# A trunk of two layers on one core: outputs turned in another PSUM bank, seven query buffers, and a norm by Sqrt

## The chip, the cores and the metric

The kernel runs on one core of a Trainium2 chip. A core has a matrix engine (TensorE, PE in the profile; PEld is its load of weights), a vector engine (VectorE, DVE), a scalar engine (ScalarE, ACT), GpSimd (POOL) and an engine whose queue issues most DMAs (SyncE, SP). Each engine runs its own queue in order; semaphores tie the queues together. Matrix products land in PSUM, which has eight banks of 128 x 512 fp32; everything else lies in SBUF. The metric is the device time of one launch in microseconds (us), as the median of several runs.

## The reference

One sequence of 512 tokens, 1024 channels, fp32, goes through two layers.

```python
# layer 0
h = rmsnorm(x, norm_mix[0])
x = x + hgrn2_mixer(h, ...)                 # gated linear recurrence, 8 heads of 128 x 128
x = x + conv_ffn(rmsnorm(x, norm_ffn[0]))   # up 1024 -> 5632, causal conv of 3, silu gate, down 2816 -> 1024
# shared keys and values
kv = rmsnorm(x, kv_norm) @ kv_w
# layer 1
h = rmsnorm(x, norm_mix[1])
x = x + diff_attention(h, k, v, ...)        # 8 heads, two softmaxes each: p1 - lam * p2
x = x + conv_ffn(rmsnorm(x, norm_ffn[1]))
return rmsnorm(x, final_norm)               # y = x * rsqrt(mean(x * x) + EPS) * g
```

In the mixer `q = silu(q)`, `f` is squashed into a forget gate between a learned lower bound and 1, and the head's output at a token is the sum over earlier tokens of `q . k`, each channel weighted by the product of the forget gates in between. In attention each head has two query-key products with a relative-position bias; `attn = p[0] - lam * p[1]` meets the values, and the 128 outputs of a head are normalised (`b_subln`) before the last projection.

## The kernel before

Activations are kept transposed: channels on the 128 partitions, the 512 tokens along a row, eight tiles `x0` to `x7`. An fp32 product is made of three products of a faster format: `split` (L59, L60) takes a tile apart into a high and a low part, ACT makes the high one and DVE the low one, and `mm3` (L99 to L101) issues three matrix products of up to 512 columns. So each weight block (512 KB, three buffers, fetched by SP's queue) costs a cast on ACT, a subtraction on DVE and 24 products on PE.

**The mixer** (`hgrn`) goes head by head. Each head's projections are followed by `prep`, a long run of elementwise work, almost all on DVE, that makes queries and keys decayed to the start or end of blocks of 4, 16, 32, 64 and 128 tokens. The query tiles of the last four lie in one pool with the tag "Q" and `QB` buffers (`QB` is 3). A tile of twice the block is made of the one before: ACT copies one half (L406), DVE multiplies the other by the gates' product (L407). `intra` then issues on PE the many small products of a head's blocks (L423, L425, then L430, L434, L437 for blocks of 16, 32, 64), transposes the keys (L445), makes the states (L450), and DVE gathers the parts under masks (L468, L479). ACT copies them to `scd` (L482 to L487), and the head's output is made by L490 (with `scd`) and L492 (with the 128-token query tile and the state). The order of all this is not written by hand: a scheduler sets each engine's queue from the dependences and the free buffers, so the number of buffers moves instructions.

**Attention** is written in an order by hand (`manual_schedule`). PSUM has four kinds of banks here: `mm` (2) for projections, `sc` (4) for scores, `tp` (1) for transposes, `po` (1) for a head's output. A head has four blocks of 128 queries. An iteration of the loop issues: the two score products of the block two ahead (`scores`, L976 and L977; DVE adds the bias and takes the row's extreme, L979; ACT takes the exponential, L985), one unit of projections on PE (three products of 512 columns), the softmax weights of the block one ahead on DVE (`weigh`, L1000), the transposes of the current block's weights into the bank `tp` (`turn`, L1007) with ACT's copy to `aT` (L1009), one or two more units, the product with the values (`gather`, L1020), and another unit. Once a head is complete, `close` normalises its output, and in the second block of the next head `turn_back` transposes it (L1037); ACT and DVE split the result into `yh` (L1039) and `yl` (L1040). `turn_back` uses the one `tp` bank, so the `turn` that comes after it waits until `yl` has been read out.

**The last norm** (`last_tile`) works on two halves of 256 tokens of the last tile, and PE does the second half's products while the first half is finished. `factor` makes 1/rms of the tokens, as a column of 128 tokens each, from sums of squares: an integer trick gives a start (L607), and three Newton steps on DVE follow, each of two instructions for each of two columns (L614, L617). `spread` transposes the columns to rows (L183), and `finish` multiplies the tiles, scaled beforehand on ACT by the norm's gain (`scaled`, L588), and sends them out (L640).

Of the kernel before, what the change touches and what calls it, by code (L numbers as in the profile page):

```python
# [11 lines left out]
F32 = mybir.dt.float32  # L12
F32R = mybir.dt.float32r
I32 = mybir.dt.int32
AF = mybir.ActivationFunctionType
# [6 lines left out]
D = 1024  # L22
# [2 lines left out]
DFF = 2816  # L25
KF = DFF // P
EPS = 1e-6
KB, QB = 6, 3
ORDERED = {mybir.EngineType.PE, mybir.EngineType.DVE, mybir.EngineType.Activation, mybir.EngineType.Pool}
U1, U2, U3 = 2, 3, 1  # L30
PIECES = {0: 1, 1: 3, 3: 6, 6: 8}
# [5 lines left out]
class Trunk:  # L37
# [530 lines left out]
    def last_tile(self, w_src, ys, kt, acc, out):  # L568

        nc, v, sp = self.nc, self.nc.vector, self.sp  # L570
        ws = []
        for k0 in range(0, kt, 8):
            wd = min(8, kt - k0)
            ws.append(self.weights(w_src[:, k0 * P:(k0 + wd) * P], wd * P))
        x, last = self.x, KD - 1
        t = [slice(half * 256, half * 256 + 256) for half in range(2)]
        ps = [self.bank() for _ in range(2)]
        sq = [sp.tile([P, T], F32, tag="sq", name="sq", bufs=2) for _ in range(2)]

        def product(half, ks):  # L580
            for k in ks:
                hi, lo = ws[k // 8]
                c = slice(k % 8 * P, k % 8 * P + P)
                self.mm3(ps[half][:, :256], (hi[:, c], lo[:, c]), (ys[k][0][:, t[half]], ys[k][1][:, t[half]]),
                         k == 0, k == kt - 1)

        def scaled(n, c):
            nc.scalar.activation(xg[n][:, c], x[n][:, c], AF.Identity, scale=self.gain(5, n))  # L588

        def squares(half):  # L590
            c = t[half]
            v.tensor_tensor(x[last][:, c], x[last][:, c], ps[half][:, :256], ALU.add)
            nc.scalar.activation(sq[half][:, c], x[last][:, c], AF.Square)
            scaled(last, c)

        def tmp(dt=F32):
            return sp.tile([P, 4], dt, tag="rs", name="rs", bufs=18)[:, :2]

        def sums(src, half):
            return self.sums(src, "mm", (2 * half, 2 * half + 1))[:, 2 * half:2 * half + 2]  # L600

        def factor(half):

            ss = sums(sq[half], half)
            ms, mh, i = tmp(), tmp(), tmp(I32)
            v.scalar_tensor_tensor(ms, ss, 1.0 / D, before[half], ALU.mult, ALU.add)
            v.tensor_scalar(i, ms.bitcast(I32), -0.5, float(0x5F3759DF), ALU.mult, ALU.add)  # L607
            v.tensor_scalar(mh, ms, -0.5, None, ALU.mult)
            r = i.bitcast(F32)
            for step in range(3):  # L610
                u, rn = tmp(), tmp()
                for c in range(2):
                    c = slice(c, c + 1)
                    v.scalar_tensor_tensor(u[:, c], r[:, c], mh[:, c], r[:, c], ALU.mult, ALU.mult)  # L614
                for c in range(2):
                    c = slice(c, c + 1)
                    v.scalar_tensor_tensor(rn[:, c], u[:, c], 1.5, r[:, c], ALU.add, ALU.mult)  # L617
                r = rn
            return r

        def spread(r):

            both = [self.bank() for _ in range(2)]
            for rb in both:
                for c in range(2):
                    self.by_column(rb[:, c * P:(c + 1) * P], r[:, c:c + 1])
            return both

        def finish(half, rb):
            by_pool = (KD - 2, KD - 1) if half else (KD - 3, KD - 2, KD - 1)  # L630
            rs = sp.tile([P, T], F32, tag="rbc", name="rbc_fin")
            nc.scalar.copy(rs[:, :256], rb[1][:, :256])
            y = [self.xp.tile([P, 2, 256], F32, tag="xs", name="fin", bufs=2 * KD) for _ in range(KD // 2)]
            for n in by_pool:
                nc.gpsimd.tensor_tensor(y[n // 2][:, n % 2], xg[n][:, t[half]], rs[:, :256], ALU.mult)
            for n in range(by_pool[0]):
                v.tensor_tensor(y[n // 2][:, n % 2], xg[n][:, t[half]], rb[0][:, :256], ALU.mult)
            queues = (nc.sync, nc.scalar if half else nc.sync)
            for n in range(0, KD, 2):
                queues[n // 2 % 2].dma_start(out[n:n + 2, :, t[half]].rearrange("n p t -> p n t"), y[n // 2])  # L640

        with self.tc.manual_schedule(engines=ORDERED):
            xg = [self.xp.tile([P, T], F32, tag="xs", name="xg", bufs=2 * KD) for _ in range(KD)]
            product(0, range(kt))
            for n in range(last):
                scaled(n, slice(0, T))
            squares(0)
            product(1, range(4))
            before = [tmp() for _ in range(2)]
            for half in range(2):  # L650
                v.tensor_scalar(before[half], sums(acc, half), 1.0 / D, EPS, ALU.mult, ALU.add)
            r = factor(0)
            product(1, range(4, kt - 6))
            rb = spread(r)
            finish(0, rb)
            product(1, range(kt - 6, kt))
            squares(1)
            finish(1, spread(factor(1)))


    def ffn(self, layer, xs, acc, on_tile, final=None):
# [66 lines left out]
    def attention(self, xkv, acc, on_tile):  # L728
# [3 lines left out]
        with ExitStack() as ctx:  # L732
# [292 lines left out]
            def close(h):  # L1025

                sums, r0, ms, po = heads.pop(h)
                o = self.sp.tile([P, T], F32, tag="res", name="o", bufs=1)
                me = self.sp.tile([P, 4], F32, tag="ome", name="ome")
                r = self.sp.tile([P, 4], F32, tag="or", name="or")  # L1030
                by_token = o.rearrange("p (i x) -> p i x", i=4)

                def turn_back():
                    tp = self.bank("tp")
                    for i in range(4):
                        oi = slice(i * P, (i + 1) * P)
                        nc.tensor.transpose(tp[:, oi], o[:, oi], self.ident)  # L1037
                    hi, lo = ys[h]
                    s.activation(hi, tp, AF.Identity, scale=self.subg2)  # L1039
                    v.scalar_tensor_tensor(lo, tp, self.subg2, hi.bitcast(F32), ALU.mult, ALU.subtract)  # L1040

                s.copy(o, po)
                chain.append(lambda: v.tensor_scalar(me, ms, 1.0 / P, EPS, ALU.mult, ALU.add))
                chain.extend(self.rsqrt_steps(r, me, 4))
                chain.append(lambda: v.tensor_tensor(r, r, r0, ALU.mult))
                chain.append(lambda: v.tensor_tensor(by_token, by_token, r.unsqueeze(2).broadcast_to([P, 4, P]),
                                                     ALU.mult))
                return turn_back
# [242 lines left out]
```

## Time and profile before

| | us |
|---|---|
| median of three timed runs | 1247.64 |
| lowest and highest of them | 1247.16, 1250.83 |
| the profiled execution's own time | 1250.46 |
| its span, first to last instruction | 1248.6 |
| PE busy in the span | 1230.5 |
| DVE busy | 842.9 |
| ACT busy | 576.0 |

In the span the mixer takes roughly the first 260 us, the first feed-forward layer runs to about 640, attention to about 865, the second feed-forward layer and the last norm to the end. A matrix product is counted as busy from its start to its modelled end, and several are in flight at once, so a busy PE need not be one at its peak. Where a row ends in brackets, it tells how long the engine stood idle before the instruction and which instruction's end released it. The trace gives the clock that TensorE was granted, as a share of the full one.

### The profile page before, as it was taken

Reading aid. Unit: us, or ns where it says so; the run is one execution under the profiler, and the core shown is the slowest. Engines: PE = TensorE matmul, PEld = TensorE weight load, DVE = VectorE, ACT = ScalarE, POOL = GpSimd, SP = SyncE. Lnnn points to the kernel's source line nnn. Section 1 sums busy time; section 2 is a strip of 40 time slices with the busy share of each in tenths; the row PEclk is TensorE's granted clock in tenths of the full one; section 3 lists DMA queues with packets and bytes.
Section 4 is the critical chain, followed back from the end, with each engine's and each line's share of the span. In section 5 each row is a group of like instructions: output and inputs, shape, how many; then the busy total and the mean of one; then the engine's idle time right before and its main releaser. Section 6 shows DMA issues by size and latency. Waiting matters only on the chain.

```text
span 1248.6 us, 17998 instructions
## 1 busy us (share of the span) xinstructions
PE 1230.5 (99%) x6994; PEld 1042.3 (83%) x6994; DVE 842.9 (68%) x1659; ACT 576.0 (46%) x1001; POOL 10.1 (1%) x32
## 2 busy tenths in 40 slices
PE   9999999999999999999999999999999999999997
PEld 7888898888888888888888888888888888888886
DVE  6988879686777777633356877777687777762223
ACT  6564555454444444322345666654444444442221
POOL 0000000000000000000000000000000000000001
PEclk9999999999999999999999999999999999999999
DMA  6233222232333332333323322213232332333322
GB/s 231 69 86 121 86 62 75 69 106 98 100 88 99 102 99 89 91 94 101 100 86 114 90 85 68 86 68 94 90 105 88 99 101 99 89 91 95 104 81 68
DMA packets 39613, 117.46 MB, mean 94 GB/s; under 512 B 4280, under 2 KB 10216, under 8 KB 39528
## 3 DMA queue, kind: packets, MB, share of 16 engines
q1 hardware_dynamic: 38488, 115.37, 29.9%
q8 instruction: 55, 0.90, 0.3%
q10 hardware_dynamic: 1040, 0.94, 0.2%
q14 instruction: 30, 0.25, 0.1%
HBM read 112.09 MB, written 3.68 MB: 93 GB/s over the span
## 4 chain that ended last, share of the span: by engine, by line
PE 62%; issue 30%; DVE 5%; ACT 2%; DMA 1%; POOL 0%; SPq 0%; POOLq 0%; ACTq 0%; DVEq 0%
PE mm L101 18%; PE mm L99 18%; PE mm L100 17%; PE po L1020 1%; DVE wlo L60 1%; PE tp L1007 1%; PE sc L99 1%; PE sc L100 1%; PE sc L101 1%; PE sc L977 1%; PE sc L976 1%; PE at L490 1%; DVE wlo L772 0%; DMA raw<-in_w_fqg_dram 0%; DVE sc L979 0%
## 5 line engine op out<-in xcount | busy, mean ns | idle before, releaser
L99 PE MATMUL mm<-xh,whi 128*128 128x512 f32 x944 | 371.3, 394 | 0.8 <-ACT whi L59 0.7
L100 PE MATMUL mm<-xl,whi 128*128 128x512 f32 x944 | 368.7, 391 | 0.6 <-DVE xl L63 0.5
L101 PE MATMUL mm<-xh,wlo 128*128 128x512 f32 x944 | 368.1, 390 | 0.0
L60 DVE TENSOR_TENSOR wlo<-wst,whi 128x1024 fp32r<-128x1024 f32 (+1 forms) x172 | 206.3, 1202 | 146.3 <-ACT whi L59 144.1
L59 ACT CAST whi<-wst 128x1024 fp32r<-128x1024 f32 (+1 forms) x172 | 177.1, 1033 | 240.4 <-PE mm L100 185.3
L100 PEld LDWEIGHTS mm<-xl,whi 128*128 128x128 f32 x944 | 177.6, 188 | 37.6 <-DVE xl L63 2.1
L99 PEld LDWEIGHTS mm<-xh,whi 128*128 128x128 f32 x944 | 177.6, 188 | 37.4 <-ACT whi L59 1.3
L101 PEld LDWEIGHTS mm<-xh,wlo 128*128 128x128 f32 x944 | 177.4, 188 | 37.0 <-DVE wlo L60 0.2
L99 PE MATMUL mm<-hh,whi 128*128 128x512 f32 (+1 forms) x374 | 141.0, 377 | 0.0
L100 PE MATMUL mm<-hl,whi 128*128 128x512 f32 (+1 forms) x374 | 140.8, 377 | 0.0
L101 PE MATMUL mm<-hh,wlo 128*128 128x512 f32 (+1 forms) x374 | 140.8, 376 | 0.0
L679 DVE TENSOR_TENSOR u<-mm,rbc_f 128x512 f32<-128x512 f32 x88 | 60.2, 688 | 73.4 <-PE mm L101 73.4
L99 PEld LDWEIGHTS mm<-hh,whi 128*128 128x128 f32 x374 | 70.4, 188 | 13.0
L100 PEld LDWEIGHTS mm<-hl,whi 128*128 128x128 f32 x374 | 70.4, 188 | 13.0
L101 PEld LDWEIGHTS mm<-hh,wlo 128*128 128x128 f32 x374 | 70.4, 188 | 12.7
L681 ACT ACTIVATE c<-u,pack 128x512 f32<-128x512 f32 x88 | 71.5, 817 | 7.5 <-DVE u L679 3.6
L59 ACT CAST hh<-c 128x512 fp32r<-128x512 f32 x44 | 27.3, 619 | 103.0 <-DVE c L690 103.0
L99 PE MATMUL mm<-whi,xh 128*128 128x256 f32 x248 | 71.7, 289 | 0.0
L101 PE MATMUL mm<-whi,xl 128*128 128x256 f32 x248 | 70.2, 283 | 0.0
L100 PE MATMUL mm<-wlo,xh 128*128 128x256 f32 x248 | 70.0, 282 | 0.0
L683 DVE SCALAR_TENSOR_TENSOR c<-u,pack,c 128x512 f32<-128x512 f32 x88 | 66.1, 751 | 2.7
L682 DVE SCALAR_TENSOR_TENSOR c<-u,pack,c 128x512 f32<-128x512 f32 x88 | 65.4, 745 | 0.0
(280 smaller groups left out, 1691.4 us busy)
## 6 DMA issues: line engine op xcount, KB each, us to landing
wst<-in_w_up_dram SPq DMA_DIRECT2D x88, 512.0 KB, 3.6
wst<-in_w_down_dram SPq DMA_DIRECT2D x32, 512.0 KB, 3.5
wst<-in_w_fqg_dram SPq DMA_DIRECT2D x21, 512.0 KB, 3.8
wst<-in_w_kq_dram SPq DMA_DIRECT2D x16, 512.0 KB, 3.6
wst<-in_w_down_dram SPq DMA_DIRECT2D x16, 384.0 KB, 3.1
wst<-in_w_i_dram SPq DMA_DIRECT2D x8, 512.0 KB, 3.9
wst<-in_w_ao_dram SPq DMA_DIRECT2D x8, 512.0 KB, 4.3
wst<-in_w_v_dram SPq DMA_DIRECT2D x8, 512.0 KB, 3.6
```

Of the source, the lines that this page charges most:

```text
L59: i = nc.scalar.copy(hi, x)
L60: j = nc.vector.tensor_tensor(lo, x, hi.bitcast(F32), ALU.subtract)
L99: mm(out, s[0], m[0], start=start, stop=False)
L100: mm(out, s[0], m[1], start=False, stop=False)
L101: mm(out, s[1], m[0], start=False, stop=stop)
L490: mm(ch(po, j), vh(j), sct[:, j], start=True, stop=(j == 0))
L679: v.tensor_tensor(u[:, 2:], ps, rb, ALU.mult)
L681: s.activation(c, u[:, 2:], AF.Identity, bias=self.cb[:, layer, n:n + 1], scale=w(2))
L682: v.scalar_tensor_tensor(c, u[:, 1:T + 1], w(1), c, ALU.mult, ALU.add)
L683: v.scalar_tensor_tensor(c, u[:, 0:T], w(0), c, ALU.mult, ALU.add)
L976: mm(sc[c], qs[h][:, c, oi], ks[h][0][:, c, 0:n], start=True, stop=False)
L977: mm(sc[c], qs[h][:, c, oi], ks[h][1][:, c, 0:n], start=False, stop=True)
```

## The change

Three edits, of which the first and the third replace code and the second is a number.

- `turn_back` takes a bank of the kind `sc` instead of the one `tp` bank. The four `sc` banks go round in turn, two to each block of scores; a head's `turn_back` takes one in between.
- `QB` goes from 3 to 7, so that a head's four query tiles and three of the next head's fit at once.
- `factor` no longer starts from the integer trick: ACT takes the square root of the mean square plus epsilon, a column at a time (`Sqrt` with its scale and bias), DVE takes the reciprocal, and one Newton step follows. `before` (the part of the sum that the first seven tiles give) gets a companion `minus`, made once. A `Sqrt` of one column of the finished `acc` stands at the head of the block, which makes ACT load that function's table there. `scaled` of the last tile moves behind `factor`.

```diff
-KB, QB = 6, 3
+KB, QB = 6, 7
...
             v.tensor_tensor(x[last][:, c], x[last][:, c], ps[half][:, :256], ALU.add)
             nc.scalar.activation(sq[half][:, c], x[last][:, c], AF.Square)
-            scaled(last, c)
...
             ss = sums(sq[half], half)
-            ms, mh, i = tmp(), tmp(), tmp(I32)
-            v.scalar_tensor_tensor(ms, ss, 1.0 / D, before[half], ALU.mult, ALU.add)
-            v.tensor_scalar(i, ms.bitcast(I32), -0.5, float(0x5F3759DF), ALU.mult, ALU.add)
-            v.tensor_scalar(mh, ms, -0.5, None, ALU.mult)
-            r = i.bitcast(F32)
-            for step in range(3):
-                u, rn = tmp(), tmp()
-                for c in range(2):
-                    c = slice(c, c + 1)
-                    v.scalar_tensor_tensor(u[:, c], r[:, c], mh[:, c], r[:, c], ALU.mult, ALU.mult)
-                for c in range(2):
-                    c = slice(c, c + 1)
-                    v.scalar_tensor_tensor(rn[:, c], u[:, c], 1.5, r[:, c], ALU.add, ALU.mult)
-                r = rn
-            return r
+            root, r, mh, u, rn = (tmp() for _ in range(5))
+            cols = [slice(c, c + 1) for c in range(2)]
+            for c in cols:
+                nc.scalar.activation(root[:, c], ss[:, c], AF.Sqrt, scale=1.0 / D, bias=before[half][:, c])
+            v.scalar_tensor_tensor(mh, ss, -0.5 / D, minus[half], ALU.mult, ALU.add)
+            v.reciprocal(r, root)
+            for c in cols:
+                v.scalar_tensor_tensor(u[:, c], r[:, c], mh[:, c], r[:, c], ALU.mult, ALU.mult)
+            for c in cols:
+                v.scalar_tensor_tensor(rn[:, c], u[:, c], 1.5, r[:, c], ALU.add, ALU.mult)
+            return rn
...
         with self.tc.manual_schedule(engines=ORDERED):
+            nc.scalar.activation(tmp()[:, 0:1], acc[:, 0:1], AF.Sqrt)
...
-            before = [tmp() for _ in range(2)]
+            before, minus = [tmp() for _ in range(2)], [tmp() for _ in range(2)]
             for half in range(2):
                 v.tensor_scalar(before[half], sums(acc, half), 1.0 / D, EPS, ALU.mult, ALU.add)
+                v.tensor_scalar(minus[half], before[half], -0.5, None, ALU.mult)
             r = factor(0)
+            scaled(last, t[0])
...
-            finish(1, spread(factor(1)))
+            r = factor(1)
+            scaled(last, t[1])
+            finish(1, spread(r))
...
                 def turn_back():
-                    tp = self.bank("tp")
+                    tp = self.bank("sc")
```

Since the mixer's order is made by the scheduler, the number of query buffers moves instructions there. On DVE, in the middle of the fourth head's masked copies (L468, `sd_379`), the products that make the fifth head's tiles of 64 and 128 tokens (`q_1557`, `q_1565`) now stand:

```order
 L468 COPY_PREDICATED sd_379<-mask,at 128x4x12
 L409 TENSOR_TENSOR k_1566<-k_1558,tot_1563 128x4x64
+L407 TENSOR_TENSOR q_1557<-q_1549,tot_1555 128x8x32
 L468 COPY_PREDICATED sd_379<-mask,at 128x4x8
-L454 SCALAR_TENSOR_TENSOR S<-S,tot_1286,at 128x128
-L497 TENSOR_TENSOR ge<-mm,rbc_n_366 128x512
+L407 TENSOR_TENSOR q_1565<-q_1557,tot_1563 128x4x64
 L468 COPY_PREDICATED sd_379<-mask,at 128x4x4
 L468 COPY_PREDICATED sd_379<-mask,at 128x4x12
```

Before, they stood among the sixth head's first products (L353 to L355), the second of them behind the fifth head's own first masked copy. So it is in most heads: both products came forward.

On PE, between the fourth head's output (L490, L492) and the fifth head's block products (L423), five products of a projection now stand that stood ahead of L490:

```order
 L490 MATMUL at<-scd_377,vt 128x128
 L492 MATMUL at<-q_1280,S 128x128
+L100 MATMUL mm<-xl_252,whi 128x512
+L101 MATMUL mm<-xh_251,wlo 128x512
+L99 MATMUL mm<-xh_263,whi 128x512
+L100 MATMUL mm<-xl_264,whi 128x512
+L101 MATMUL mm<-xh_263,wlo 128x512
 L423 MATMUL at<-r_1512,k_1506 32x80
 L425 MATMUL at<-r_1528,k_1524 32x48
```

In the other heads L490 moves as well: five products of 256 columns later in the first head, one of them earlier in the third, four of 512 columns earlier in the seventh.

On ACT, at the end of the last layer, the seven scalings (L588) stood one behind each tile's square (L143); now they stand together behind the table load and the first `Sqrt`:

```order
+L638 ACT_TABLE_LOAD
+L638 ACTIVATE rs<-acc 128x1
 L588 ACTIVATE xg<-x_72,gains 128x512
...
 L588 ACTIVATE xg<-x_78,gains 128x512
 L593 ACTIVATE sq<-x_79 128x256
+L607 ACTIVATE rs<-mm,rs 128x1 x2
 L588 ACTIVATE xg<-x_79,gains 128x256
```

In attention nothing moves; only the bank that L1037 writes and L1039 and L1040 read has another name.

## The prediction

> **What bounds the kernel now.** I read the page first, then the table by stretches of time, then the rows of TensorE in order of time wherever a stretch was not full.
>
> ```profile
> span 1248.6 us, 17998 instructions
> PE 1230.5 (99%) x6994; PEld 1042.3 (83%) x6994; DVE 842.9 (68%) x1659; ACT 576.0 (46%) x1001; POOL 10.1 (1%) x32
> ```
>
> TensorE (PE) has something in flight for 99% of the span, so time can only be won where its queue stands still or its clock is low. The next rows (columns: stretch, its length, busy us and count of PE, PEld, DVE, ACT, POOL; granted clock; DMA share; GB/s) are four stretches in which that happens, and one of the feed-forward layer for scale.
>
> ```profile
> 149.05:151.00 1.95, 0.00 (x1) 0.03 (x1) 1.95 (x4) 1.26 (x4) 0.00 (x0) 1.00 0.34 32
> 151.06:154.47 3.41, 3.41 (x16) 2.90 (x17) 3.41 (x11) 1.11 (x3) 0.00 (x0) 0.50 0.35 139
> 797.10:799.07 1.97, 0.01 (x2) 0.01 (x1) 1.64 (x4) 1.95 (x5) 0.00 (x0) 1.00 0.60 133
> 799.60:803.01 3.41, 3.41 (x10) 2.63 (x9) 2.09 (x4) 1.19 (x5) 0.00 (x0) 0.50 0.04 8
> 525.00:550.00 25.00, 25.00 (x112) 20.69 (x111) 8.63 (x11) 7.33 (x9) 0.00 (x0) 1.00 0.35 101
> ```
>
> In the full stretch 112 products of 512 columns take 25 us: 0.22 us each, with no gap. At 149 us (the mixer) and at 797 us (attention) PE does nothing for 1.95 us, and each time the granted clock is 0.50 for the 3.41 us that follow, which costs another 1.7 us. What ended the waits stands in PE's own rows (start, length, instruction, idle time before it and its releaser):
>
> ```profile
> 148.66 0.39 PE L434 MATMUL at<-q,k 128*32 128x32 f32 x13
> 151.00 0.50 PE L437 MATMUL at<-q,k 128*64 128x64 f32 x3 [1.95 <-DVE q L407]
> ...
> 704.96 0.40 PE L101 MATMUL mm<-xqh,wlo 128*128 128x512 f32 x1
> 705.64 0.33 PE L1007 MATMUL tp<-pack,at 128*128 128x128 f32 x1 [0.29 <-DVE yl L1040]
> ...
> 750.37 0.40 PE L101 MATMUL mm<-xqh,wlo 128*128 128x512 f32 x1
> 751.99 0.33 PE L1007 MATMUL tp<-pack,at 128*128 128x128 f32 x1 [1.23 <-DVE yl L1040]
> ...
> 796.71 0.40 PE L101 MATMUL mm<-xqh,wlo 128*128 128x512 f32 x1
> 799.07 0.33 PE L1007 MATMUL tp<-pack,at 128*128 128x128 f32 x1 [1.96 <-DVE yl L1040]
> ```
>
> The mixer's wait is for a query tile (L407). The three in attention are for `yl` (L1040), the last reader of the one "tp" bank, which the next block's transposes (L1007) need. From start to start less 0.23 for the product between, attention loses 0.45, 1.39 and 2.13 us: 3.97. The mixer loses 1.95.
>
> **The change part by part.** *The bank.* `turn_back` now writes an "sc" bank, so L1007 no longer waits for `yl`. What is late next shows around the longest of the waits:
>
> ```profile
> 793.79 0.69 ACT L985 ACTIVATE p<-sc,stat 128x512 f32<-128x512 f32 x1 [1.69 <-DVE stat L979]
> ...
> 797.55 0.68 ACT L1039 ACTIVATE yh<-tp,subg 128x512 fp32r<-128x512 f32 x1
> 798.12 1.04 ACT L769 CAST whi<-wst 128x1024 fp32r<-128x1024 f32 x1
> 799.71 0.48 ACT L1009 COPY aT<-tp 128x384 f32<-128x384 f32 x1 [0.55 <-PE tp L1007]
> ...
> 795.28 0.28 PE L976 MATMUL sc<-kh,qs 128*128 128x128 f32 x1
> ```
>
> The transposes can then start at 796.94. But ACT runs in order, and its copy `aT` stands behind `yh` and a weight's cast, which ends at 799.16; with 0.48 for the copy, `gather` (L1020) has its operand at 799.64. PE reaches it after 0.3 us of transposes and six products, at 798.6. So about 1.0 of the 2.13 us comes back as a wait for `aT`. At 751 us `yh` is ACT's last piece of work before the copy and nothing stands between, so I keep the 1.39 whole, and 0.45 at 705. Net 3.0 us; between 0.45 (both long waits only move to `aT`) and 3.97.
>
> The price is paid by "sc", four banks in turn: after a `turn_back` the second half of the next scores takes the bank that the exponentials of the scores just before it read. That exponential starts at 793.79 and ends with its sum by 794.7; the scores that would take its bank issue at 795.28. So 0.6 us are left, and I cost this at nothing; if the DVE's row maxima were 0.6 us later, it would be a wait.
>
> *The query tiles.* A head makes four of them (16, 32, 64, 128); with three buffers the third and fourth must wait for the previous head's last use (L492):
>
> ```profile
> L407 DVE TENSOR_TENSOR q<-q,tot 128x256 f32<-128x256 f32 x24 | 10.8, 451 | 5.4 <-PE at L492 5.4
> L406 ACT COPY q<-q 128x256 f32<-128x256 f32 x24 | 9.7, 404 | 14.7 <-PE at L492 9.8 <-PE at L430 2.9 <-DVE q L397 1.1
> ...
> 70.96 0.36 ACT L487 COPY scd<-at 64x256 f32<-64x256 f32 x1
> ...
> 71.42 0.35 PE L490 MATMUL at<-scd,vt 128*128 128x128 f32 x1 [1.28 <-issue]
> ...
> 121.90 0.36 ACT L487 COPY scd<-at 64x256 f32<-64x256 f32 x1
> ...
> 122.54 0.50 PE L490 MATMUL at<-scd,vt 128*128 128x128 f32 x3
> ...
> 222.72 0.37 ACT L487 COPY scd<-at 64x256 f32<-64x256 f32 x1
> ...
> 224.61 0.49 PE L490 MATMUL at<-scd,vt 128*128 128x128 f32 x3
> ```
>
> With seven, the scheduler puts both products of a head into the chain of masked copies (L468) of the head before it, as the order above shows, well before L437 asks for them. I take the whole 1.95 us off. Against it: these two products now stand ahead of L479 and of the copies L482 to L487 that L490 waits for. In the first head that is two times 0.45 us, while five 256-column products (0.12 each by the rows' spacing, 0.6 in all) move ahead of L490: the wait there, now 1.28, grows by 0.3. In the third head one of the two was in the chain already, so 0.45 is added; L490 has 122.54 less 122.26, that is 0.28, to spare, and moves up by one 256-column product: another 0.3. The seventh has 1.52 to spare and gives up four products of 0.22: still enough. Net 1.95 - 0.6 = 1.35 us; between 0 (the wait moves to L490) and 1.95.
>
> *The clock.* Both waits that were followed by 3.41 us at 0.50 lasted 1.95 us; those of 1.23 and 1.28 us were not followed by it. After the change the longest I expect are 1.6 and 1.0, so I count both stretches gone: 2 x 1.7 = 3.4 us; between 1.7 (the first head's wait trips it now) and 3.4. The Trainium skill, "TensorE: Matmul & The Clock Gate", section "What's actually happening", has the clock fall only after an idle window of about 3.4 us, and the windows free-running. By the first half no wait here would cost clock at all, and this term would be nothing; the trace disagrees, 1.95 us were enough. By the second the same wait trips it in one run and not in another.
>
> *The last norm.* The second half's 1/rms runs alone at the end. Rows of the tail, and of the nearest kin of the new operations:
>
> ```profile
> 1240.11 0.16 DVE L606 SCALAR_TENSOR_TENSOR rs<-mm,rs 128x2 f32<-128x2 f32 x1 [1.21 <-PE mm L178]
> ...
> 1241.49 0.34 DVE L614 SCALAR_TENSOR_TENSOR rs<-rs 128x1 f32<-128x1 f32 x2
> 1241.75 0.28 DVE L617 SCALAR_TENSOR_TENSOR rs<-rs 128x1 f32<-128x1 f32 x2
> ...
> L743 ACT ACTIVATE lme<-mm 128x2 f32<-128x2 f32 x1 | 0.2, 172 | 0.0
> L1023 ACT ACTIVATE sq<-po,r 128x128 f32<-128x128 f32 x32 | 11.8, 368 | 12.3 <-PE po L1020 9.1 <-issue 2.8
> L996 DVE RECIPROCAL r<-sums 128x1 f32<-128x1 f32 x32 | 5.0, 156 | 0.0
> L743 ACT ACT_TABLE_LOAD x1 | 1.3, 1283 | 0.0
> L588 ACT ACTIVATE xg<-x,gains 128x512 f32<-128x512 f32 x7 | 5.0, 709 | 0.0
> ...
> 1222.16 0.71 ACT L588 ACTIVATE xg<-x,gains 128x512 f32<-128x512 f32 x1
> 1229.32 0.42 ACT L593 ACTIVATE sq<-x 128x256 f32<-128x256 f32 x1 [6.46 <-DVE x L592]
> ```
>
> Now: 1240.11 to 1242.03, 1.92 us. Then: two Sqrt of one column, 0.17 each by the exponential of two columns out of PSUM (bounds 0 and 0.37), a reciprocal 0.16, one Newton step 0.54 (1241.49 to 1242.03), and some 0.15 for two hand-overs: 1.2. It gains 0.7 us (0.3 to 1.0). The table load (1.28) and the seven scalings, which now all stand behind it and behind the finished `acc`, need 1.28 + 7 x 0.71 = 6.25 us from 1222.16 on, to 1228.4; ACT's next work comes at 1229.32, so its idle 6.46 us cover them with 0.9 to spare, and what ran over would delay the first half's square by as much. "ScalarE: Activation LUTs" of the Trainium skill, section "Rules for kernel authors", budgets 0.3 us for an ACTIVATE; by it this term would be 0.45 us, an estimate.
>
> *The sum.* 3.0 + 1.35 + 3.4 + 0.7 = 8.45 us off the profiled execution's 1250.46 us (span 1248.6 and 1.9 around it): 1242.0. That execution lies 2.8 us over the median of the timed runs (1247.64; 1247.16 to 1250.83), close to the slowest of them. Two stretches of half clock cost 3.4 us, which is also the distance between the slowest timed run and the other two. I take it that the fast ones had none: 1247.64 - 3.0 - 1.35 - 0.7 = 1242.6. I forecast 1242.2, 0.44% less. What can be told from no change here is about 0.3%, or 3.7 us.
>
> **The rivals.** *The attention wait only moves.* If ACT, not the bank, is what is late, PE waits for `aT` at L1020 instead, all but 0.45 us of it, and the half clock after 799 us stays: 1250.46 - 0.45 - 1.35 - 1.7 - 0.7 = 1246.3. For it: ACT's cast ahead of the copy at 798. Against it: at 751 us nothing stood there.
>
> *More buffers do nothing.* DVE is busy for all of 149.05 to 151.00, so the query product may have been late because DVE was, not because of its buffer. Then 1.95 us and its clock stay: 1250.46 - 3.0 - 1.7 - 0.7 = 1245.1. Against it: the 5.4 and 9.8 us that L407 and L406 waited for L492, and the new order.
>
> *The timed runs had the half clock as well*, and the 2.8 us are the profiler's: 1247.64 - 8.45 = 1239.2. For it: the waits are in every run. Against it: the spread of the runs.
>
> *Slower: the masked chain becomes late.* Each product of the query chain needs the copy before it (L406 on ACT), and DVE runs in order; if DVE has to stand for ACT, a head's chain is late by x, not by 0.45. Heads one, three and seven then lose x - 0.6 (on top of 1.28), x - 0.16 and x - 0.62. At x = 1.7 (two products of 0.45 and two copies of 0.40 end to end) that is 1.1 + 1.5 + 1.1 and one stretch of half clock, 5.4 us in place of the 0.6 counted: 1247.0, no change. From x = 2.4 on all three waits pass 1.7 us and trip the clock: 1.8 + 2.2 + 1.8 + 5.1 = 10.9, and the time is 1252.5. Against it: in the new order other instructions of DVE (L468, L409) stand between these products, under which a copy of 0.40 us hides.
>
> **How the numbers follow.** Forecast 0.62 (own range 1239.5 to 1244.5); moved wait 0.16; no effect of the buffers 0.09; half clock in the timed runs 0.06; late chain 0.07. The range runs from the third rival to the first: 1238.5 to 1246.5; outside are the late chain and the far ends, some 0.15. Faster by over 0.3% means under 1243.9: 0.59 of the forecast's 0.62, 0.02 of the second rival's and the 0.06 give 0.67; the rest of these, with the moved wait, 0.26; slower 0.07.
>
> **What would show it.** The bank: no idle time at L1007 released by `yl`, and at most a wait near 1 us at L1020 for `aT`; wrong if the scores (L976) wait for ACT. The buffers: no wait for L492 in L407's group, none at L437; L490's waits decide between forecast and the last rival. The clock: no stretch at 0.50 before the tail; one after 70 us would cost 1.7. The norm: from the last L178 to L183 some 1.2 us instead of 1.92. Above 1244 with all these right, the time went into a wait that I have not named.

## The result

The changed kernel takes 1240.57 us (median of 4 runs, 1240.24 to 1240.92). The kernel before took 1248.22 us in the runs beside it (1247.16 to 1250.83). The ratio is 0.9931, 95% interval 0.992 to 0.9943: 0.7% faster. The forecast was 1242.2 us, range 1238.5 to 1246.5, and "faster by over 0.3%" had 0.67.

The profiled execution of the changed kernel took 1240.69 us, 9.77 us less than that of the kernel before. Its page, the engines' busy time and the chain that ended last, with the chain of the kernel before as the last row:

```profile
span 1238.4 us, 18006 instructions
PE 1227.0 (99%) x6994; PEld 1040.1 (84%) x6994; DVE 840.8 (68%) x1643; ACT 578.0 (47%) x1007; POOL 10.0 (1%) x32
PE 96%; DVE 1%; ACT 1%; DMA 0%; issue 0%; SPq 0%; ACTq 0%; DVEq 0%
...
PE 62%; issue 30%; DVE 5%; ACT 2%; DMA 1%; POOL 0%; SPq 0%; POOLq 0%; ACTq 0%; DVEq 0%
```

TensorE (PE) does the same 6994 products and is now nearly the whole chain. ("issue" is time for which the profile shows nothing that was waited for.) DVE and ACT had 7% of the chain and have 2%. The longest waits of PE that the profile lists for this kernel (us in total, how many, the longest):

```profile
PE at L490 <- issue: 1.3, 1, 1.3
PE mm L183 <- DVE rs L613: 1.2, 1, 1.2
PE mm L178 <- ACT sq L593: 1.0, 1, 1.0
PE at L250 <- POOL ones L212: 1.0, 1, 1.0
```

The waits at L1007 for `yl` and the one at L437 for a query tile are gone, and no wait of their size has come up elsewhere; the two that follow in the list, at the start and ahead of the second feed-forward product, come to 0.8 us. What remains was there before.

**The bank.** Where the longest wait stood, PE, ACT and DVE now show, in order of time:

```profile
790.87 0.49 PE L1007 MATMUL tp<-pack,at 128*128 128x128 f32 x3
791.48 0.68 ACT L1039 ACTIVATE yh<-sc,subg 128x512 fp32r<-128x512 f32 x1
792.05 1.05 ACT L769 CAST whi<-wst 128x1024 fp32r<-128x1024 f32 x1
792.19 0.75 DVE L1040 SCALAR_TENSOR_TENSOR yl<-sc,subg,yh 128x512 fp32r<-128x512 f32 x1 [0.30 <-ACT yh L1039]
792.98 0.49 ACT L1009 COPY aT<-tp 128x384 f32<-128x384 f32 x1
793.52 0.74 PEld L1020 LDWEIGHTS po<-vt,aT 128*128 128x128 f32 x6 [0.51 <-ACT aT L1009]
```

The transposes (790.87) no longer wait for `yl`, which is written only at 792.19. `aT` is late, as predicted, behind `yh` and the cast: it ends at 793.47, and the products of `gather` start at 793.52. From the last product before them (793.05) this is 0.47 us where such a step otherwise takes 0.23, so PE loses 0.24 us there. The attention stage lost 3.97 us to these waits and now loses 0.24: 3.73 us gained.

**The query tiles.** PE in the head that had waited, the two groups that had waited for L492, and the first head's L490 with the copy that it needs:

```profile
148.41 0.44 PE L434 MATMUL at<-q,k 128*32 128x32 f32 x15
148.78 0.68 PE L437 MATMUL at<-q,k 128*64 128x64 f32 x8
...
L407 DVE TENSOR_TENSOR q<-q,tot 128x256 f32<-128x256 f32 x24 | 10.5, 436 | 0.0
L406 ACT COPY q<-q 128x256 f32<-128x256 f32 x24 | 9.7, 404 | 6.2 <-DVE q L407 5.2 <-DVE q L397 0.9
...
71.31 0.36 ACT L487 COPY scd<-at 64x256 f32<-64x256 f32 x1
71.78 0.68 PE L490 MATMUL at<-scd,vt 128*128 128x128 f32 x4 [1.30 <-issue]
```

L437 follows L434 without idle time, neither group waits for L492, and L490 waits 1.30 us where it waited 1.28. From start to start, the gap from L434 to L437 was 2.02 us too long (1.95 of it idle); all of that is gained.

**The norm.** The tail of the second half, first in the kernel before and then in the changed one, and the table load at its beginning:

```profile
1239.46 0.61 PE L178 MATMUL mm<-ones,sq 128*128 128x1 f32 x4 [1.02 <-ACT sq L593]
1241.96 0.67 PE L183 MATMUL mm<-pack,rs 128*128 128x128 f32 x4 [1.89 <-DVE rs L617]
...
1230.01 0.60 PE L178 MATMUL mm<-ones,sq 128*128 128x1 f32 x4 [1.02 <-ACT sq L593]
1230.66 0.41 ACT L607 ACTIVATE rs<-mm,rs 128x1 f32<-128x1 f32 x2 [0.70 <-PE mm L178]
1231.18 0.15 DVE L609 RECIPROCAL rs<-rs 128x2 f32<-128x2 f32 x1
1231.63 0.28 DVE L613 SCALAR_TENSOR_TENSOR rs<-rs 128x1 f32<-128x1 f32 x2
1231.84 0.66 PE L183 MATMUL mm<-pack,rs 128*128 128x128 f32 x4 [1.23 <-DVE rs L613]
...
1212.82 1.28 ACT L638 ACT_TABLE_LOAD   x1
1214.22 4.39 ACT L588 ACTIVATE xg<-x,gains 128x512 f32<-128x512 f32 x7
1219.88 0.42 ACT L593 ACTIVATE sq<-x 128x256 f32<-128x256 f32 x1 [1.27 <-DVE x L592]
```

From L178 to L183 it is 1.83 us; before it was 2.50 (1239.46 to 1241.96). That is 0.67 us gained. The scalings end at 1218.61, and ACT is idle for 1.27 us before the square that follows: the load is covered.

**The clock.** No stretch at 0.50 lies between the start and the tail. Before there were two, at 1.7 us each. The terms add to 3.73 + 2.02 + 0.67 + 3.4 = 9.82 us; the two profiled executions differ by 9.77. That the two agree to 0.05 us is in part chance: the spans differ by 10.2 us, and about 0.3 us of this lies ahead of everything that the change touches (the first layer's product that starts at 7.97 us before starts at 7.70 now).

### The profile page after: what moved, and what is told of

It is laid out like the page before. It is cut to its first block, busy times and chain, and to the rows that moved or that the text cites. A ratio compares the mean times of both kernels' runs of the same rounds, so it can differ in the third digit from the quotient of the medians.

```text
span 1238.4 us, 18006 instructions
## 1 busy us (share of the span) xinstructions
PE 1227.0 (99%) x6994; PEld 1040.1 (84%) x6994; DVE 840.8 (68%) x1643; ACT 578.0 (47%) x1007; POOL 10.0 (1%) x32
## 4 chain that ended last, share of the span: by engine, by line
PE 96%; DVE 1%; ACT 1%; DMA 0%; issue 0%; SPq 0%; ACTq 0%; DVEq 0%
PE mm L99 28%; PE mm L100 28%; PE mm L101 28%; PE po L1020 1%; PE sc L977 1%; PE sc L99 1%; PE sc L100 1%; PE sc L976 1%; PE sc L101 1%; PE tp L1007 1%; PE at L490 1%; PE at L423 1%; PE at L492 0%; PE at L450 0%; DMA raw<-in_w_fqg_dram 0%; PE at L437 0%
```

## The experiments

Each run below gives a median of single executions; those of the kernel before beside them lie at 1249.2 (17 runs, beside the first four), 1249.04 (9, beside the next four) and 1248.52 (13, beside the last two). With the 1248.22 beside the change itself, the same kernel's median moves by up to 1.0 us from one set of runs to another, so smaller differences between medians of different sets say little.

### Each part alone

The bank alone, on the kernel before:

```diff
-                    tp = self.bank("tp")
+                    tp = self.bank("sc")
```

> The kernel before with the bank of the turned outputs alone changed. The prediction's own terms: the waits of 3.97 us at L1007 go, and with nine products instead of six between the turn and the gathering products (the profile after has three units there, of 2, 3 and 1 tiles) about 0.25 us comes back at L1020, so 3.7 us of stalls, plus 1.7 us if the half-clock stretch in the attention stage goes with them: 1248.2 - 3.7 = 1244.5 without the clock, 1242.8 with it. Its trace then has no row at L1007 that waits for yl, no 0.50 clock event near 730 to 850 us, and the query waits at L437 as before (1.95 us). Rival, that the wait only moves to L1020: 1248.2 - 0.5 = 1247.7, with rows at L1020 that wait about 3.5 us in all.

Measured: 1244.12 us (1243.32 to 1245.21, 4 runs), ratio 0.9952 (0.9937 to 0.9967). PE's longest waits in its profile:

```profile
PE at L437 <- DVE q L407: 1.9, 1, 1.9
...
PE at L490 <- issue: 1.2, 1, 1.2
```

There is no row at L1007 or L1020. The rival of a wait that only moves (1247.7) falls. As expected, no half-clock stretch is left in attention; the one in the mixer stayed, at 151.46 us behind L437. The median is nearer to the value without the clock's share (1244.5) than to the one with it (1242.8).

The seven buffers alone:

```diff
-KB, QB = 6, 3
+KB, QB = 6, 7
```

> The kernel before with seven buffers of query tiles instead of three and nothing else. The prediction's terms: 1.95 us of waits at L437 less up to 0.6 that comes back at L490, plus 1.7 us if the mixer's half-clock stretch goes: 1246.9 to 1246.3 without the clock, 1245.2 to 1244.6 with it. Since the profile after showed no growth at L490, its own reading is 1248.2 - 1.95 - 1.7 = 1244.5. Rival, that the buffers do nothing because the products wait for the same producers elsewhere: 1248.2, with the idle time of L490 grown by what L437 lost.

Measured: 1245.34 us (1244.98 to 1246.66, 5 runs), ratio 0.9967 (0.9954 to 0.9981). Of its waits:

```profile
PE tp L1007 <- DVE yl L1040: 3.5, 3, 2.0
...
PE at L490 <- issue: 1.3, 1, 1.3
```

L437 is out of the list and L490 hasn't grown. The rival, that the buffers do nothing, falls; the time is just above the expected values with the clock's share (1244.6 to 1245.2) and under those without (1246.3 to 1246.9).

The norm alone (the change without its first and its last pair of lines):

```diff
-            r = i.bitcast(F32)
-            for step in range(3):
...
+                nc.scalar.activation(root[:, c], ss[:, c], AF.Sqrt, scale=1.0 / D, bias=before[half][:, c])
+            v.reciprocal(r, root)
```

> The kernel before with the changed norm of the tail alone. By the prediction's term 0.7 us less: 1247.5, which hardly shows in the times; in the trace the step from the last L178 to the first L183 is 1.2 us where it was 1.9, and the waits at L1007 and L437 and both half-clock stretches stand as before. Rival, that the table load and the seven scalings behind it reach past the point where their last result is wanted: a row at L178 or L183 that waits for ACT, and 1248 or more.

Measured: 1248.73 us (1246.13 to 1249.78, 10 runs), ratio 0.9991 (0.9981 to 1.0): by the times alone no gain could be claimed. The waits carry the verdict:

```profile
PE tp L1007 <- DVE yl L1040: 3.5, 3, 2.0
PE at L437 <- DVE q L407: 1.9, 1, 1.9
...
PE mm L183 <- DVE rs L613: 1.2, 1, 1.2
```

L183 waits 1.2 us where the kernel before shows 1.89 (in the rows of the norm above), and nothing waits for the table load. One point of the expectation missed: both waits stand, but in this execution neither was followed by a stretch at half clock. That made the clock a question of its own.

Four buffers in place of three:

```diff
-KB, QB = 6, 3
+KB, QB = 6, 4
```

> The kernel before with four buffers of query tiles instead of three. If the wait at L437 is a matter of the rotation by one head alone, four buffers end it as seven do, and this run is within 0.4 us of the run with seven (1244.5 by its reading). Rival, that with four the fifth head's tile still waits for the last products of the head before: a part of the 1.95 us stays in rows at L437, and the time lies between that run and 1248.2.

Measured: 1246.32 us (1245.02 to 1246.98, 7 runs). PE's list of waits has no row at L437, and the same first three as with seven buffers, with the same numbers (L1007 3.5, L183 1.9, L490 1.3). One more buffer ends the wait at L437; the other three do nothing for it. The medians differ by 1.0 us, more than the 0.4 expected, though the fastest runs agree (1245.02 and 1244.98). The profiled execution had a half-clock stretch at 794.81 us, after the third wait at L1007, which that with seven buffers did not have; that the clock makes the whole difference of the medians is likely by this, but not shown.

### The parts taken off again, and the clock

The clock's records in these profiles have a pattern. In the kernel before, the first stretch at full clock lasted 146.773 us, the one between the two slow stretches 645.119 us, and a slow stretch 3.413 us: the first is 43 times the last, the second 189 times. In the other profiles too every such stretch is a whole number of times 3.413 us. So I laid windows of 3.413 us from the first moment at full clock through each execution. The columns of the next rows are those of the prediction's table by stretches; the third number is PE's busy time in the window. The kernel before, the windows that hold its two long waits:

```profile
147.63:151.04 3.41, 1.46 (x109) 1.38 (x99) 3.41 (x7) 1.97 (x5) 0.00 (x0) 1.00 0.37 89
796.16:799.57 3.41, 1.45 (x9) 0.93 (x8) 2.68 (x9) 2.95 (x6) 0.00 (x0) 1.00 0.45 111
```

The next window after each of them is the slow one (151.05 and 799.58 us). The same rows for the one slow window with the bank alone (after L437) and with four buffers (after L1007), of one execution each:

```profile
148.04:151.45 3.41, 1.47 (x85) 1.38 (x73) 3.41 (x7) 2.30 (x5) 0.00 (x0) 1.00 0.35 83
...
791.39:794.80 3.41, 1.44 (x7) 0.87 (x6) 2.39 (x7) 3.21 (x6) 0.00 (x0) 1.00 0.54 136
```

The slow windows begin at 151.46 and 794.81 us. The kernel with the norm alone, the same two waits:

```profile
147.48:150.89 3.41, 1.54 (x112) 1.42 (x104) 3.41 (x7) 1.90 (x4) 0.00 (x0) 1.00 0.40 100
...
796.01:799.42 3.41, 1.89 (x10) 1.64 (x11) 3.07 (x11) 2.81 (x9) 0.00 (x0) 1.00 0.35 77
```

Here the end of the first wait falls into the next window, and the other is cut in two at 796.0 us. PE is busy for 1.54 us or more in each, and the clock stays at 1.00 throughout. With seven buffers the longest wait at L1007 is cut as well, at 795.1 us, and no slow window follows:

```profile
791.70:795.11 3.41, 1.77 (x10) 1.18 (x8) 2.39 (x4) 2.79 (x6) 0.00 (x0) 1.00 0.60 171
```

So, for these waits, it is not the length that decides but how much of it falls into one window: PE stood idle for 1.94 us or more in the windows that the slow clock followed, and for 1.87 us or less in the others. (The expectation below counts the same waits a little longer, as 2015 and 1948 ns.) This was a theory made from these profiles, and the two runs that take a part off the change were to test it. Three buffers again, the rest as changed:

```diff
-KB, QB = 6, 7
+KB, QB = 6, 3
```

> The changed kernel with three buffers of query tiles again, the bank and the norm as changed. If the parts add, the 1.95 us at L437 come back: 1242.5 where no half-clock stretch follows, and 1244.2 where one does. The clock's theory from the runs before: stretches begin on a grid of 3.413 us that runs freely from the first full-clock moment, and one comes when PE stood still for about 2.0 us within one window of the grid (2015 ns or more was followed by one, 1948 ns or less was not). By it the single times lie in two groups 1.7 us apart, the profiled run is in the slower one only if at least 2.0 us of the wait at L437 fall within one window, and the stretch then starts with the next window. Rival, that the clock follows the wait's length alone: all runs in one group.

Measured: 1242.59 us (1242.10 to 1244.14, 5 runs), ratio 0.9954 (0.9939 to 0.9969). The single times are 1242.10, 1242.25 and 1242.59 with a mean clock of 0.998, and 1243.82 and 1244.14 with 0.996: two groups, 1.7 us apart, where the change itself spread over 0.7 us. The profiled execution was one of the slower:

```profile
148.14:151.55 3.41, 1.46 (x70) 1.31 (x59) 3.41 (x6) 2.30 (x5) 0.00 (x0) 1.00 0.34 89
151.56:154.97 3.41, 3.41 (x10) 2.73 (x10) 3.41 (x12) 0.80 (x2) 0.00 (x0) 0.50 0.22 85
```

The whole wait lies in one window, PE is busy for 1.46 us of the window, and the next one runs at 0.50. The old bank again, the rest as changed:

```diff
-                    tp = self.bank("sc")
+                    tp = self.bank("tp")
```

> The changed kernel with the turned outputs back in the bank of their own kind, the buffers and the norm as changed. If the parts add, the waits at L1007 (3.97 us over the nominal steps) come back and the 0.24 at L1020 goes: 1240.6 + 3.7 = 1244.3 without a half-clock stretch, 1246.0 with one, which only the third wait, of 2.12 us, is long enough for. Rival, that part of the gain came from the interplay of bank and buffers, since both change PE's place against the chain: below 1243.5 or above 1246.5. The sum of the parts, taken off the changed kernel one by one, should be that of the parts put on the kernel before one by one.

Measured: 1245.52 us (1244.44 to 1246.66, 10 runs), ratio 0.9975 (0.9965 to 0.9985). Five of the ten lie from 1244.44 to 1245.18, five from 1245.86 to 1246.66. The groups are less sharp here: 0.7 us lie between them, and both have runs with a mean clock of 0.997. The profiled execution, one of the slower ones:

```profile
793.05:796.46 3.41, 1.45 (x9) 0.97 (x8) 3.04 (x11) 2.84 (x7) 0.00 (x0) 1.00 0.35 79
796.47:799.88 3.41, 3.41 (x12) 2.85 (x11) 1.55 (x2) 0.72 (x5) 0.00 (x0) 0.50 0.16 41
```

Both expectations held, and the rival that the wait's length alone sets the clock falls: with three buffers the same wait gave both speeds in runs of the same kernel. An estimate from the rows: an idle stretch of 1.94 us lies whole within one window of 3.41 us at (3.41 - 1.94) / 3.41 = 43% of all positions, and 2 of 5 and 5 of 10 runs were in the slower group.

PE's busy time is not the whole rule, though. At the end of the program, with seven buffers alone and with the old bank, the windows that start at 1232.02 and 1233.38 us have PE busy for 1.82 and 1.96 us, more than two windows above that kept the clock, and the slow clock follows both. The products there are others (of 256 columns and of single ones); what is counted stays open.

Where the stalls are compared without the clock, the parts add: the median of the faster group lies 1.7 us over the changed kernel for the buffers (1242.25 - 1240.57; 2.02 by the rows) and 4.15 for the bank (1244.72 - 1240.57; 3.73 by the rows), so no interplay of more than some 0.4 us shows.

### The units of work ahead of the gather

```diff
-U1, U2, U3 = 2, 3, 1
+U1, U2, U3 = 2, 2, 2
```

> The changed kernel with one unit of the attention's filler work moved from ahead of the gathering products to behind them (2, 2, 2 in place of 2, 3, 1), so that six products in place of nine stand between the turn and the gather. If the wait at L1020 that the change left is only what these products don't cover (ACT copies aT behind a weight's cast), it grows by the three products, 0.68 us, at the place near 793 us where it was 0.24, to about 0.9, and the median is 1241.2. This is the 1.0 that the prediction put there with its count of six. Rival, that other blocks lean on these products too: several of the 32 gathers then wait, and the time rises by more, 2 us and above.

Measured: 1242.39 us (1242.14 to 1242.71, 4 runs), 1.8 us more than the change, nearer to the rival. PE's rows at the place and one block later:

```profile
792.88 0.94 PE L1020 MATMUL po<-vt,aT 128*128 128x128 f32 x6
...
798.13 0.39 PE L100 MATMUL mm<-wlo,xh 128*128 128x256 f32 x1 [0.45 <-DVE wlo L772]
...
800.64 1.05 PE L1020 MATMUL po<-vt,aT 128*128 128x128 f32 x7 [0.93 <-ACT aT L1009]
```

The gather at 792.88 shows no idle time of PE, where 0.9 us was expected. Moving the unit moved the weight's cast as well, from ahead of ACT's copy to behind it (the cast now starts at 795.78, the copy at 792.35). What was lost is lost one block later, in a wait for a weight and one for `aT`. So this run shows that the third unit carries more than one deadline; it can't confirm the 0.24 us, which rest on the rows of the changed kernel.

### The table load

```diff
-            nc.scalar.activation(tmp()[:, 0:1], acc[:, 0:1], AF.Sqrt)
```

> The changed kernel without the one leading Sqrt of the tail, so that the table is loaded at the first factor, near 1222.0 us in the trace after. The factor's last result there is at 1223.3 and is wanted at 1226.25; with the load of 1.28 us it comes at 1224.6, so by the theory that the load is covered twice over nothing changes: 1240.6, within 0.3. Rival, that the load holds up work on the path (the copy at L627 or the first four products of L183): up to 1.3 more, 1241.9. If the table has to be loaded again for the second factor, 1.3 to 2.6 more.

Measured: 1240.43 us (1240.21 to 1241.13, 4 runs), against 1240.57: no change. ACT in the tail:

```profile
1221.04 1.28 ACT L607 ACT_TABLE_LOAD   x1 [1.08 <-DVE rs L646]
1222.33 0.41 ACT L607 ACTIVATE rs<-mm,rs 128x1 f32<-128x1 f32 x2
1226.55 0.37 ACT L627 COPY rbc_fin<-mm 128x256 f32<-128x256 f32 x1 [3.40 <-PE mm L183]
```

The load starts 1.5 us after the square of this half (L593, 1219.53) and ends at 1222.32. From the square to the Sqrt it is now 2.80 us where the changed kernel shows 2.16, so half of the load lies under the wait for the sums and half comes later, and 3.40 us of ACT's idle time stand behind it. There is no second load. The leading Sqrt buys nothing measurable here.

### What is left at L490, and a faster version

```diff
-                for g in range(4):
-                    row = slice(32 * g, 32 * g + 32)
-                    s.copy(sct[row, :, 32 * g:32 * g + 32], sdt[row])
                 for g in range(2):
                     row = slice(64 * g, 64 * g + 32)
                     s.copy(sct[row, :, 64 * g + 32:64 * g + 64],
                            pb[row, 64:192].rearrange("p (c o) -> p c o", c=4))
                 s.copy(sct[0:64, :, 64:128], pb[0:64, 192:448].rearrange("p (c o) -> p c o", c=4))
+                for g in range(4):
+                    row = slice(32 * g, 32 * g + 32)
+                    s.copy(sct[row, :, 32 * g:32 * g + 32], sdt[row])
```

> The changed kernel with ACT's three copies at L485 and L487 put ahead of its four copies at L482, since they wait for nothing that DVE has still to write. In the trace after, L482 starts at 69.55 when DVE ends L479, and the copies behind it end at 71.67, where the products of L490 in the first head start. Ended by L482's 1.22 us alone they could start at about 70.8 in place of 71.78: the wait of 1.30 us falls to about 0.4 and the median to 1239.7. Rival, that the wait is set by something else, since the profile names no releaser for it: 1240.6. If the copies then come before the products that they read are done, the first ones wait and nothing is gained.

Measured: 1240.67 us (1240.41 to 1240.98, 4 runs): nothing gained. ACT's rows of the first head (in this kernel L482 and L484 are the moved copies, L487 the four from `sd`):

```profile
69.89 0.52 ACT L482 COPY scd<-at 32x128 f32<-32x128 f32 x2 [2.48 <-DVE sd L479]
70.42 0.36 ACT L484 COPY scd<-at 64x256 f32<-64x256 f32 x1
70.69 1.21 ACT L487 COPY scd<-sd 32x128 f32<-32x128 f32 x4
```

In both kernels L490 starts 0.11 us after ACT's last copy has ended (71.67 to 71.78 in the changed kernel, 71.90 to 72.01 here), so the copies are what it waits for, though the profile names no releaser. The moved copies start no earlier: the first is released by DVE's L479, as the four were. L479 reads the same PSUM bank, and it stands ahead of the copy in the program; that this order of two readers is kept was not tried by itself, so the cause stays open. The expectation's second way of failing is the one that came, with another partner than it named.

The Newton step left out as well:

```diff
-            v.scalar_tensor_tensor(mh, ss, -0.5 / D, minus[half], ALU.mult, ALU.add)
             v.reciprocal(r, root)
-            for c in cols:
-                v.scalar_tensor_tensor(u[:, c], r[:, c], mh[:, c], r[:, c], ALU.mult, ALU.mult)
-            for c in cols:
-                v.scalar_tensor_tensor(rn[:, c], u[:, c], 1.5, r[:, c], ALU.add, ALU.mult)
-            return rn
+            return r
...
-                v.tensor_scalar(minus[half], before[half], -0.5, None, ALU.mult)
```

> The copies moved as in the run before, and in the norm of the tail the Newton step left out: the factor is the reciprocal of ACT's square root, with its rounding as it comes. The step is 0.35 us at L611 and 0.28 at L613, from 1231.37 to 1231.91 in the trace after, so the wait of 1.23 us at L183 falls to 0.7. With the copies: 1240.6 - 0.9 - 0.5 = 1239.2. Rival, that DVE's chain wasn't the last thing that L183 waited for: no gain over the run with the copies alone.

Measured: 1239.62 us (1239.55 to 1239.77, 5 runs), ratio to before 0.9924 (0.9911 to 0.9936). All five lie under all runs of the change (from 1240.24) and of the run with the copies alone (from 1240.41). In its profile:

```profile
1230.90 0.17 DVE L608 RECIPROCAL rs<-rs 128x2 f32<-128x2 f32 x1 [1.65 <-ACT rs L607]
1231.12 0.65 PE L183 MATMUL mm<-pack,rs 128*128 128x128 f32 x4 [0.70 <-DVE rs L608]
```

The wait of 1.23 us is 0.70, as expected: 0.53 us. The medians differ by 1.05 from the run with the copies alone. In the profiled executions 0.42 us of the difference stands at the program's start, where the two kernels don't differ (the first layer's product at 7.99 us there starts at 7.57 here), so about 0.5 us is what the Newton step can be credited with. It beats both kernels, at the price of the factor's last bits.

## Why the prediction was right

**The mechanisms held, and two sizes were too small.** The forecast was 1.6 us above the measured median, with a range 8 us wide. By the prediction's own steps, in us:

| step | predicted | measured | from |
|---|---|---|---|
| bank | 3.0 | 3.73 | 3.97 at L1007, 0.24 left at L1020 |
| query tiles | 1.95 - 0.6 | 2.02 - 0.02 | start to start at L437; L490 1.28 to 1.30 |
| clock, in the profiled execution | 3.4 | 3.4 | two stretches at 0.50, none after |
| norm | 0.7 | 0.67 | L178 to L183, 2.50 to 1.83 |

**The bank.** The copy `aT` was late by the very instructions named. It ended at 793.47, 6.2 us earlier than the 799.64 worked out in the old timing; some 4.1 us of that were gained before the attention's first turn-back (702.21 to 698.09) and 1.8 at its two shorter waits. What failed is the count: "PE reaches it after 0.3 us of transposes and six products". Between the turn and the gather of this block stand three units, nine products; six stand between the scores and the turn. (U1, U2 and U3 are 2, 3 and 1 units: two ahead of the turn, three behind it, two in the first block of a head, and one behind the gather. The text ahead of the prediction has one, then one or two, then one.) Nine take 2.07 us in place of 1.38, so 0.24 came back, not 1.0.

The step "sc", costed at nothing with 0.6 us to spare, held: no wait of the scores (L976, L977) for ACT shows with the bank alone or in the change.

**The query tiles.** The products moved into the masked chain of the head before, and no wait came in place of L437's. The step that failed is "In the first head that is two times 0.45 us": 0.45 is the duration of one, but DVE starts its next instruction about 0.34 us after such a product (64.26 to 64.60 in the changed kernel). Set against the same place in the program (L450, 0.26 us earlier than before), ACT's last copy came 0.61 us later and PE reached L490 about 0.6 later as well: the two cancel. In the third head ACT's last copy ended at 121.98, 0.28 us earlier than before, as the whole program there was; it was no later at all, L490 started at 122.19 with no wait, and the 0.3 predicted there did not appear. DVE's rows show why: one query product (L407) that stood at 97.44 us, ahead of this head's masked chain, left that place, so the chain's first copy (L468) starts at 105.70 in place of 106.16. From there to L479 the chain grew by 0.17 us only (119.88 - 106.16 = 13.72 before, 119.59 - 105.70 = 13.89 now), since a small product (L386) moved behind it as another L407 came in. The rival "late masked chain", which priced a far larger x, does not show in any of these rows.

**The clock.** "Both stretches gone" was right. The reason given (1.95 us trips, 1.23 and 1.28 us do not) was a part of the rule only: such a wait trips it in some executions. So it was luck that the profiled execution before had caught both windows; in that of the norm alone the same two waits caught none. "I take it that the fast ones had none" fits, though the clocks of those very runs are not on record: of the 39 runs of the kernel before beside the experiments (1246.18 to 1251.29, median 1249.07), the six with a mean clock of 0.998 have a median of 1247.09 (1246.18 to 1248.85). From there the stalls alone, 3.73 + 2.0 + 0.67 = 6.4, lead to 1240.7; measured 1240.57. The rest of the gain in the medians goes to the slow windows that the kernel before has more often than not: 1249.07 - 1247.09 = 2.0 us in the typical run, as far as six runs can tell. The rival that all timed runs had both stretches in full would have given 1239.2, below every run of the change.

The prediction weighed the Trainium skill here ("TensorE: Matmul & The Clock Gate", section "What's actually happening"). Its free-running window of 3413 ns agrees with every stretch in these profiles. Its condition of an idle window of about 3.4 us does not, if it means a window idle throughout: windows in which PE was busy for 1.44 to 1.47 us of 3.41 were followed by the slow clock.

**The norm.** The trace shows 0.67 us of the 0.7 expected. The times agree as far as they go: the three runs of the norm alone with a mean clock of 0.998 have a median of 1246.26, 0.83 under the six of the kernel before. Two Sqrt of one column took 0.41 us together; 0.34 had been taken from the neighbouring row. By the 0.3 us that the Trainium skill's "ScalarE: Activation LUTs", section "Rules for kernel authors", budgets for an ACTIVATE the estimate was 0.45; the trace is nearer to the row's price. The load and the scalings were covered with 1.27 us to spare where 0.9 had been worked out, since the scalings start 0.6 us apart and not 0.71.

## What to carry to other kernels

Price a wait that "comes back" by counting the instructions between the two places in the engine's own rows, not in the code's description, and price short instructions by the distance of their starts, not by their durations: the misses in the bank's term and in the first head are of these two kinds. When a kernel's times fall into groups, look for a wait near the length that costs clock: removing it takes away the wait in every run, and the slow window in those runs that caught it. A buffer count is worth testing one step at a time; here, on the kernel before, the fourth ended the wait at L437 as seven did.

## What the runs showed of the hardware

- The granted clock of TensorE is decided by windows of 3.413 us that don't follow the program: the first moment at full clock lies 4.1 to 6.6 us after the first instruction, different in each execution. In six windows of five profiled executions PE was busy for 1.44 to 1.47 us, and each was followed by one window at 0.50; windows with 1.54, 1.77 and 1.89 were not. Two windows at the end of programs, with other products and 1.82 and 1.96 us busy, were, so busy time alone is not the measure. A wait of 2.0 us in these layers therefore costs 1.7 us more, or nothing, by where it falls: 3 of 5 and 5 of 10 runs were in the faster group where one such wait was left.
- A slow window costs 1.7 us: the two groups of the run with three buffers lie 1.7 us apart (1242.25 and 1243.98 in the middle).
- A table load of 1.28 us, left where it falls, delayed its Sqrt by 0.64 us only (2.80 after the square in place of 2.16), since it began while the sums were still on their way.
- An ACT copy out of a PSUM bank was released, by the profile, by a DVE instruction that only read the same bank (L479, the copy at 69.89 us), and the gain expected of reordering the copies did not come. Whether the chip asks for this order or the program does is not shown.
